# Splitting attention operands into hi and lo when they are made, not when they are loaded

## The chip, the cores and the metric

The kernel runs on one core of a Trainium2 chip. The metric is the device time of one execution in microseconds (us). The engines are named as the profile names them: PE multiplies matrices (PEld is its weight load), DVE is the vector engine, ACT the scalar engine, POOL is GpSimd, and SP only issues DMAs. Each engine works through its own instructions in a fixed order; an instruction that waits holds up all that stand behind it on the same engine, and this holds for SP and its DMAs too.

## What is computed

Two layers of a decoder trunk on 1024 tokens of width 1024. In each layer one input projection feeds four branches, which are gated, projected, merged by sigmoid gates, and added to the residual. Cut to the parts that the change touches:

```
q = (rms_norm(c_q) @ w_uq).reshape(S, 8 heads, 96)          # 64 plain + 32 rotary
k_nope, v = split((rms_norm(c_kv) @ w_ukv).reshape(S, 8, 128), 64)
k = concat(k_nope, k_rope shared by the heads)               # 96
q, k = rope(rms_norm(q)), rope(rms_norm(k))
y_b = causal softmax(q k^T / sqrt(96)) v                     # 8 heads, 1024 x 1024
# memory attention: 4 heads of 64, 256 memory tokens
q_m = rms_norm(h @ w_mq);  k_m, v_m = split(rms_norm(mem) @ w_kv)
y_m = softmax(q_m k_m^T / 8) v_m
```

## The kernel before

All data are fp32. A matrix product is taken in three fp32r passes: each operand x is split into hi = x rounded to fp32r and lo = x - hi, and the sum hi·hi + lo·hi + hi·lo is accumulated in PSUM. The helper `split` (L106 is its ACT copy that makes hi, L96 the subtraction that makes lo) does that on ACT plus either DVE or POOL. Where the source is a PSUM tile with a gain, ACT applies the gain and DVE makes lo in one scalar-tensor-tensor instruction.

The stages of a layer run in this order: statistics and the kv latent, memory queries (`mq_stage`), state-space input, `v_stage` and `k_stage` (keys and values of the latent attention), the state-space scan (`s5_scan`; `su` is its input read back from DRAM, `sz` and `sx` its DVE steps), memory keys and values, the state-space GLU (`gch`, `gcl` are its split operands, `glu` its result), `mem_attention` (4 heads), the q latent and `q_stage`, `attention` (8 heads in 4 blocks of 256 queries), and the merges.

Keys, queries, values and memory queries go through DRAM to change their layout. Before, each is stored as plain fp32 (`kscr`, `q2scr`, `vscr`, `qscr`), loaded into a raw tile `wr`, and split after each load: `fetch` makes `fh`/`fl` for keys and `wh`/`wl` for queries (hi on ACT, lo on POOL), `load_head` splits the values in the same way, and `mem_q` loads the same 64 rows twice, makes hi of both halves on ACT, and subtracts in the lower half on DVE. A head is loaded once per layer, three query blocks ahead.

Beside this, each layer has 18 background blocks (`background`, marked `bg` on PE): 48 matmuls of 128x512 each, 864 per layer, for the merge gates and branch gates. Their weights go through a raw tile `br` of which there is one, are converted by DVE (`bh`) and POOL (`bl`), and the product is taken up by DVE into `bgx`. Their loads and splits are ahead of the rest by priority (offset -800), and their matmuls have the lowest priority (offset -100000), so that a scheduler, which fixes the order of each engine when the kernel is built, puts them where it finds nothing else ready. Thus a change of any stage also changes where these matmuls stand. SP issues all DMAs.

In `k_stage` a small chain (`fk`, transposed by PE, through DRAM as `rkscr`) gives the factor tiles `rkb`, by which DVE multiplies the four key tiles `kraw`; POOL makes the rotary part `kro`, PE transposes it, ACT copies it out as `krt`; then all goes to `kscr`.

Of the kernel before, what the change touches and what calls it, by code (L numbers as in the profile page):

```python
# [17 lines left out]
P = 128  # L18
D = 1024
S = 1024  # L20
# [24 lines left out]
class Trunk:  # L45
# [174 lines left out]
    def setup(self):  # L220
# [37 lines left out]
        self.gscr = self.dp.tile([2, P, S], F32, name="gscr")  # L258
        self.qscr = self.dp.tile([2, P, S], F32, name="qscr")
        self.xscr = self.dp.tile([8, P, S], F32, name="xscr")  # L260

        self.kscr = self.dp.tile([96, 8, S], F32, name="kscr")
        self.vscr = self.dp.tile([8, P, 8, 64], F32, name="vscr")
        self.q2scr = self.dp.tile([96, 8, S], F32, name="q2scr")
        self.rkscr = self.dp.tile([64, P], F32, name="rkscr")
# [490 lines left out]
    def mq_stage(self, l):  # L756

        nc = self.nc
        ssm, sqs = self.ss(32, "ssm"), []
        for p in range(2):  # L760
            ps = self.cm(l, B_MQ + p, self.xg)
            sq = self.U("mqsq")
            self.act(sq, ps, AF.Square)
            q = self.U("mq")
            self.ts(q, ps, self.gmq[:, l:l + 1], MUL)
            nc.sync.dma_start(out=self.qscr[p], in_=q)
            sqs.append(sq)
        v = self.turn(self.quad([(self.sel2, sqs[i % 2][:, i // 2 * 512:i // 2 * 512 + 512]) for i in range(4)]))
        for i in range(4):
            nc.vector.tensor_copy(ssm.rearrange("p (u t h) -> p u t h", u=2, t=4)[:, i // 2, :, 2 * (i % 2):2 * (i % 2) + 2], v[:, :, 32 * i:32 * i + 2])  # L770
        pre = self.ss(32, "pre")
        nc.vector.tensor_copy(pre.rearrange("p (t h) -> p t h", t=8), self.rs.unsqueeze(2).to_broadcast([P, 8, 4]))
        r = self.inv_rms(ssm, 32, 64, pre)
        self.mqs = self.lp.tile([P, 32], F32, tag="mqs", name=self._n("mqs"))
        self.ts(self.mqs, r, M_SCALE, MUL)
# [93 lines left out]
    def q_stage(self, l, qacc):  # L869
# [4 lines left out]
        g = [t[:, l:l + 1] for t in (self.gq_x1, self.gq_x2)]  # L874
        dst = self.q2scr
        ps1 = self.block(w(0), self.cq, 6)
# [13 lines left out]
        for x, o in enumerate((o1, o2)):  # L890
            nc.sync.dma_start(out=dst[64 + 16 * x:80 + 16 * x].rearrange("f h s -> (f h) s"), in_=o)

# [10 lines left out]
        for p in range(4):  # L903
            ps = self.block(w(2 + p), self.cq, 6)
            sq = self.U("qsq")
            self.act(sq, ps, AF.Square)
            q = self.U("q")
            self.ts(q, ps, self.gqk[:, l:l + 1], MUL)
            for hh in range(2):
                nc.sync.dma_start(out=dst[0:64, 2 * p + hh], in_=q[hh * 64:hh * 64 + 64])  # L910
            sums(*sqs[p], first=p == 0)
# [24 lines left out]
    def v_stage(self, l):  # L936
# [3 lines left out]
        for t in range(8):  # L940
            ps = self.tr()
            xsl = slice(t * P, (t + 1) * P)
            for kt in range(2):
# [4 lines left out]
                self.mmr(ps, xh[:, xsl], wl[:, wsl], False, kt == 1)  # L948
            vt = self.U("vt")
            self.ts(vt[:, 0:512], ps, self.bkv[:, t:t + 1], MUL)  # L950
            nc.sync.dma_start(out=self.vscr[:, :, t, :].rearrange("h p d -> p h d"), in_=vt[:, 0:512].rearrange("p (h d) -> p h d", h=8))

    def k_stage(self, l, between):
# [44 lines left out]
        for x in range(2):  # L998
# [3 lines left out]
                    rk.rearrange("p (h t) -> p t h", h=8).unsqueeze(2).to_broadcast([P, 8, 16, 8]), MUL, eng=nc.gpsimd)  # L1002
            kt = self.U("krt")
            for tg in range(2):
                pt = self.tr()
                for j in range(4):
                    t = 4 * tg + j
                    nc.tensor.transpose(pt[:, j * P:(j + 1) * P], kro[:, t * P:(t + 1) * P], self.ident)
                self.act(kt[:, tg * 512:(tg + 1) * 512], pt, AF.Copy)
            nc.sync.dma_start(out=self.kscr[64 + 16 * x:80 + 16 * x].rearrange("f h s -> (f h) s"), in_=kt)  # L1010
        for p in range(4):
            self.tt(kraw[p], kraw[p], rbs[p], MUL)
            for hh in range(2):
                nc.sync.dma_start(out=self.kscr[0:64, 2 * p + hh], in_=kraw[p][hh * 64:hh * 64 + 64])  # L1014

# [10 lines left out]
    def load_head(self, h):  # L1026
        k = self.fetch(self.kscr[:, h])
        raw, v = self.wraw(), self.U("v", F32R)
        raw = raw[:, 0:512]
        self.nc.sync.dma_start(out=raw, in_=self.vscr[h].rearrange("p t d -> p (t d)"))  # L1030
        vv = v.rearrange("p (t k d) -> p k t d", t=8, k=2)
        self.split(vv[:, 0], vv[:, 1], raw.rearrange("p (t d) -> p t d", t=8), sub_eng=self.nc.gpsimd)
        return k, v

    def load_q(self, h):
        return self.fetch(self.q2scr[:, h], self.wpair())

# [95 lines left out]
    def mem_q(self, head):  # L1133

        nc = self.nc
        raw, q = self.wraw(), self.U("mq", F32R)
        hs = slice(head % 2 * 64, head % 2 * 64 + 64)
        for k in range(2):
            nc.sync.dma_start(out=raw[k * 64:k * 64 + 64], in_=self.qscr[head // 2, hs])
        self.act(q, raw, AF.Copy)  # L1140
        self.tt(q[64:128], raw[64:128], q[64:128].bitcast(F32), SUB)
        return q
# [532 lines left out]
```

## Time and profile before

| | us |
|---|---|
| median of three runs | 2448.62 (2446.93 to 2453.8) |
| the profiled execution | 2454.93 |
| its span, first to last instruction | 2453.0 |
| PE busy in it | 2338.4 (95%) |
| DVE, POOL, ACT busy | 1220.7, 776.5, 708.6 |

The mean granted PE clock of the profiled execution is 0.986 of 2.4 GHz. A row of the timeline gives the start, the duration, the engine, line and operation, out<-in, the count, and in brackets the idle time ahead of it with what ended that idle time. PE is busy nearly all the time, so its order and the waits in it are what is to be read.

### The profile page before, as it was taken

The page shows a single profiled execution, that of the slowest core. Times are in us where ns is not written, and L with a number is a line of the kernel's source. Part 1 is how long each engine was busy: PE and PEld are TensorE (multiplying, and loading weights), DVE is VectorE, ACT ScalarE, POOL GpSimd, SP SyncE. Part 2 cuts the span into 40 slices and gives each one's busy share as a digit, 9 for nine tenths or more (in the row PEclk, how much of TensorE's full clock was granted, in tenths as well). Part 3 has the DMA queues.
Part 4 walks back from the last instruction along what each step waited for, and adds up shares of the span by engine and source line. Part 5 has one row for each costly group of instructions (what it writes and reads, how often), then busy time and mean ns, then how long its engine had stood idle before and what let it go on. Part 6 is the DMA issues. An engine that isn't in the chain of part 4 may idle for free. (4 is left out here: it accounts for less than half of the span.)

```text
span 2453.0 us, 28729 instructions
## 1 busy us (share of the span) xinstructions
PE 2338.4 (95%) x11494; PEld 1885.2 (77%) x11494; DVE 1220.7 (50%) x1839; ACT 708.6 (29%) x1201; POOL 776.5 (32%) x606
## 2 busy tenths in 40 slices
PE   7998888999999999999999889999999999999999
PEld 5766677868788887887876667787778888788877
DVE  6454783266766224236244557714666652333341
ACT  3121253147753101101111213612577420111010
POOL 3533112432214124342445421233322132234411
PEclk9999999999999999999999999999999999999999
DMA  4226343242331113222432363313323211222342
GB/s 151 74 94 182 115 137 101 82 114 87 94 109 36 52 52 95 69 78 102 155 105 71 95 183 126 119 60 103 112 83 104 85 43 52 73 74 78 103 155 69
DMA packets 91701, 237.59 MB, mean 97 GB/s; under 512 B 25200, under 2 KB 34352, under 8 KB 91568
## 3 DMA queue, kind: packets, MB, share of 16 engines
q1 hardware_dynamic: 91568, 235.76, 30.1%
q8 instruction: 90, 1.47, 0.3%
q14 instruction: 43, 0.35, 0.0%
HBM read 175.27 MB, written 60.46 MB: 96 GB/s over the span
## 5 line engine op out<-in xcount | busy, mean ns | idle before, releaser
L96 POOL TENSOR_TENSOR wl<-wr,wh 128x1024 fp32r<-128x1024 f32 (+3 forms) x125 | 297.7, 2382 | 949.6 <-DVE wh L152 635.1
L152 DVE CAST wh<-wr 128x1024 fp32r<-128x1024 f32 (+2 forms) x110 | 79.1, 719 | 630.1 <-PE mm L176 555.3
L176 PE MATMUL mm<-xh,wh 128*128 128x512 f32 x1216 | 379.5, 392 | 10.1 <-ACT xh L106 9.7
L176 PE MATMUL mm<-xh,wl 128*128 128x512 f32 x1216 | 376.8, 391 | 0.7 <-POOL wl L96 0.7
L176 PE MATMUL mm<-xl,wh 128*128 128x512 f32 x1216 | 377.3, 391 | 0.0
L176 PEld LDWEIGHTS mm<-xh,wh 128*128 128x128 f32 x1216 | 227.8, 189 | 61.8 <-ACT xh L106 9.7
L176 PEld LDWEIGHTS mm<-xh,wl 128*128 128x128 f32 x1216 | 228.6, 188 | 49.9 <-POOL wl L96 1.6
L176 PEld LDWEIGHTS mm<-xl,wh 128*128 128x128 f32 x1216 | 228.9, 188 | 49.1 <-issue 0.8
L176 PE MATMUL bg<-xh,bh 128*128 128x512 f32 x576 | 228.1, 414 | 14.8 <-DVE bgx L96 14.8
L176 PE MATMUL bg<-xl,bh 128*128 128x512 f32 x576 | 225.8, 410 | 0.0
L176 PE MATMUL bg<-xh,bl 128*128 128x512 f32 x576 | 223.2, 407 | 0.6 <-POOL bl L96 0.5
L96 POOL TENSOR_TENSOR bl<-br,bh 128x1024 fp32r<-128x1024 f32 x36 | 95.3, 2647 | 309.0 <-DVE bh L152 209.9
L106 ACT ACTIVATE cmn<-cmn,bmh 128x1024 f32<-128x1024 f32 x44 | 50.7, 1152 | 457.2 <-DVE cmn L96 457.2
L176 PEld LDWEIGHTS bg<-xh,bh 128*128 128x128 f32 x576 | 111.9, 195 | 43.9 <-DVE bgx L96 23.3
L96 DVE TENSOR_TENSOR pT<-tr,pT 128x512 fp32r<-128x512 f32 x192 | 128.1, 686 | 30.7 <-ACT pT L106 28.5
L176 PE MATMUL pv<-pT,v 128*128 128x256 f32 x640 | 134.3, 308 | 7.3 <-DVE pT L96 3.8
L176 PEld LDWEIGHTS bg<-xh,bl 128*128 128x128 f32 x576 | 111.1, 193 | 24.4 <-issue 3.2
L176 PEld LDWEIGHTS pv<-pT,v 128*128 128x128 f32 x640 | 98.2, 190 | 40.1 <-DVE pT L96 14.5
L176 PEld LDWEIGHTS bg<-xl,bh 128*128 128x128 f32 x576 | 111.3, 194 | 21.4 <-issue 4.0
L106 ACT ACTIVATE pT<-tr 128x512 fp32r<-128x512 f32 x192 | 109.9, 596 | 46.2 <-PE tr L1100 36.0
L1059 DVE TENSOR_REDUCE mx<-mm 128x1 f32<-128x128 f32 (+7 forms) x128 | 96.1, 753 | 51.4 <-PE mm L176 49.9
L106 ACT ACTIVATE pr<-mm,nm,qs 128x128 f32<-128x128 f32 (+7 forms) x128 | 105.5, 832 | 0.7
(452 smaller groups left out, 4226.6 us busy)
## 6 DMA issues: line engine op xcount, KB each, us to landing
wr<-in_w_cm_dram SPq DMA_DIRECT2D x76, 512.0 KB, 3.6
br<-in_w_cm_dram SPq DMA_DIRECT2D x36, 512.0 KB, 3.7
bgscr<-bgx SPq DMA_DIRECT2D x20, 512.0 KB, 4.0
gate<-bgscr SPq DMA_DIRECT2D x20, 512.0 KB, 5.9
ysscr<-bgx SPq DMA_DIRECT2D x16, 512.0 KB, 2.6
br<-ysscr SPq DMA_DIRECT2D x16, 512.0 KB, 3.6
wr<-in_w_out_dram SPq DMA_DIRECT2D x16, 512.0 KB, 3.7
bgr<-riscr SPq DMA_DIRECT2D x24, 256.0 KB, 4.9
```

The source lines that it names most:

```text
L96: (eng or self.nc.vector).tensor_tensor(out=out, in0=x, in1=y, op=op)
L106: self.nc.scalar.activation(out, x, f, **k)
L152: self.nc.vector.tensor_copy(hi[:, :n], raw)
L176: self.nc.tensor.matmul(out, lhsT, rhs, start=start, stop=stop)
L1059: nc.vector.reduce_max(out=mx, in_=ps[:, 0:n], axis=AX.X)
```

## The change

Keys, queries, values and memory queries are split when they are made. The DRAM tiles hold hi and lo, and the loads go straight into the operand tiles; `fetch` is left for the gated branches alone.

```
-        self.qscr = self.dp.tile([2, P, S], F32, name="qscr")
+        self.qscr = self.dp.tile([2, 2, P, S], F32, name="qscr")
-        self.kscr = self.dp.tile([96, 8, S], F32, name="kscr")
-        self.vscr = self.dp.tile([8, P, 8, 64], F32, name="vscr")
-        self.q2scr = self.dp.tile([96, 8, S], F32, name="q2scr")
+        self.kscr = [self.dp.tile([96, 8, S], F32, name="kscr" + x) for x in "hl"]
+        self.q2scr = [self.dp.tile([96, 8, S], F32, name="q2scr" + x) for x in "hl"]
+        self.vscr = self.dp.tile([8, P, 8, 2, 64], F32, name="vscr")
...
-            q = self.U("mq")
-            self.ts(q, ps, self.gmq[:, l:l + 1], MUL)
-            nc.sync.dma_start(out=self.qscr[p], in_=q)
+            q = self.U("mqh", F32R), self.U("mql", F32R)
+            self.split(*q, ps, gain=self.gmq[:, l:l + 1])
+            for k in range(2):
+                nc.sync.dma_start(out=self.qscr[k, p], in_=q[k].bitcast(F32))
...
         for x, o in enumerate((o1, o2)):
-            nc.sync.dma_start(out=dst[64 + 16 * x:80 + 16 * x].rearrange("f h s -> (f h) s"), in_=o)
+            part = self.U("qrh", F32R), self.U("qrl", F32R)
+            self.split(*part, o, sub_eng=nc.gpsimd)
+            for k in range(2):
+                nc.sync.dma_start(out=self.q2scr[k][64 + 16 * x:80 + 16 * x].rearrange("f h s -> (f h) s"), in_=part[k].bitcast(F32))
...
-            vt = self.U("vt")
-            self.ts(vt[:, 0:512], ps, self.bkv[:, t:t + 1], MUL)
+            vt = self.U("vt", F32R).rearrange("p (h k d) -> p k h d", h=8, k=2)
+            self.split(vt[:, 0], vt[:, 1], ps.rearrange("p (h d) -> p h d", h=8), gain=self.bkv[:, t:t + 1])
...
         for p in range(4):
             self.tt(kraw[p], kraw[p], rbs[p], MUL)
-            for hh in range(2):
-                nc.sync.dma_start(out=self.kscr[0:64, 2 * p + hh], in_=kraw[p][hh * 64:hh * 64 + 64])
+            part = self.U("kh", F32R), self.U("kl", F32R)
+            self.split(*part, kraw[p], sub_eng=nc.gpsimd)
+            for k in range(2):
+                for hh in range(2):
+                    nc.sync.dma_start(out=self.kscr[k][0:64, 2 * p + hh], in_=part[k][hh * 64:hh * 64 + 64].bitcast(F32))
...
     def load_head(self, h):
-        k = self.fetch(self.kscr[:, h])
-        raw, v = self.wraw(), self.U("v", F32R)
...
+        k, v = [self.U("k" + x, F32R) for x in "hl"], self.U("v", F32R)
+        for z, src in zip(k, self.kscr):
+            self.nc.sync.dma_start(out=z[0:96].bitcast(F32), in_=src[:, h])
+        self.nc.sync.dma_start(out=v.bitcast(F32), in_=self.vscr[h].rearrange("p t k d -> p (t k d)"))
...
     def mem_q(self, head):
-        raw, q = self.wraw(), self.U("mq", F32R)
+        q = self.U("mq", F32R)
         hs = slice(head % 2 * 64, head % 2 * 64 + 64)
         for k in range(2):
-            nc.sync.dma_start(out=raw[k * 64:k * 64 + 64], in_=self.qscr[head // 2, hs])
-        self.act(q, raw, AF.Copy)
-        self.tt(q[64:128], raw[64:128], q[64:128].bitcast(F32), SUB)
+            nc.sync.dma_start(out=q[k * 64:k * 64 + 64].bitcast(F32), in_=self.qscr[k, head // 2, hs])
         return q
```

The queries of `q_stage` get the same edit as the memory queries, and `krt` becomes the pair `krh`, `krl`. On SP the number of issues grows from 545 to 621.

The order of the engines moves with it. In the next two lists stands what POOL does around `kro` in the key stage of the first layer; `br`, `bh`, `bl` are a background block's raw, hi and lo weights. Before:

```order
L96 TENSOR_TENSOR bl_942<-br_939,bh_941 128x1024
L96 TENSOR_TENSOR kro_2113<-krot_1439,qs_2092 128x1024
L96 TENSOR_TENSOR kro_2129<-krot_1439,qs_2092 128x1024
L96 TENSOR_TENSOR bl_1003<-br_1000,bh_1002 128x1024
L96 TENSOR_TENSOR bl_1064<-br_1061,bh_1063 128x1024
```

After, on POOL at the same place:

```order
L96 TENSOR_TENSOR bl_944<-br_941,bh_943 128x1024
L96 TENSOR_TENSOR bl_1005<-br_1002,bh_1004 128x1024
L96 TENSOR_TENSOR kro_2129<-krot_1441,qs_2108 128x1024
L96 TENSOR_TENSOR kro_2149<-krot_1441,qs_2108 128x1024
L96 TENSOR_TENSOR kl_2171<-kraw_1913,kh_2170 128x1024
L96 TENSOR_TENSOR kl_2180<-kraw_1930,kh_2179 128x1024
L96 TENSOR_TENSOR kl_2189<-kraw_1947,kh_2188 128x1024
L96 TENSOR_TENSOR kl_2198<-kraw_1964,kh_2197 128x1024
L96 TENSOR_TENSOR bl_1066<-br_1063,bh_1065 128x1024
```

A second background split (bl_1005) now stands ahead of `kro`, and the next one (bl_1066) behind four new `kl`. On SP, the stores of the keys in the first layer stood before the change like this, with the scan's input `su` and the next weights `br` behind them:

```order
L1010 DMA kscr<-krt_2115 128x1024
L1010 DMA kscr<-krt_2131 128x1024
L1014 DMA kscr<-kraw_1905 64x1024 x2
L1014 DMA kscr<-kraw_1922 64x1024 x2
L1014 DMA kscr<-kraw_1939 64x1024 x2
L1014 DMA kscr<-kraw_1956 64x1024 x2
L620 DMA su_2157<-cscr 128x8x128
L149 DMA br_1000<-in_w_cm_dram 128x1024
```

After, from the first `kh` on, behind four stores of krh and krl:

```order
L1022 DMA kscrh<-kh_2170 64x1024 x2
L1022 DMA kscrl<-kl_2171 64x1024 x2
L1022 DMA kscrh<-kh_2179 64x1024 x2
L1022 DMA kscrl<-kl_2180 64x1024
L149 DMA br_1063<-in_w_cm_dram 128x1024
L1022 DMA kscrl<-kl_2180 64x1024
L1022 DMA kscrh<-kh_2188 64x1024 x2
L149 DMA br_1124<-in_w_cm_dram 128x1024
L1022 DMA kscrl<-kl_2189 64x1024 x2
L1022 DMA kscrh<-kh_2197 64x1024 x2
L1022 DMA kscrl<-kl_2198 64x1024 x2
L620 DMA su_2205<-cscr 128x8x128
```

The key stores are 20 instead of 10, two loads of background weights stand among them (another, br_1002, stands ahead of the `rkb` loads), and `su` is last. The third place is SP around the first memory query of the second layer. Before, the loads of its first two heads (`wr`) had been issued long ahead, and behind the stores of `glu` stood those of the other two:

```order
L149 DMA br_12052<-in_w_cm_dram 128x1024
L686 DMA gscr<-glu_11520 128x1024
L686 DMA gscr<-glu_11537 128x1024
L1139 DMA wr_11789<-qscr 64x1024 x2
L1139 DMA wr_11887<-qscr 64x1024 x2
```

After, where mq_11726 is the first head's query, read by the first matmul of the memory scores:

```order
L149 DMA br_12232<-in_w_cm_dram 128x1024
L1148 DMA mq_11726<-qscr 64x1024
L686 DMA gscr<-glu_11572 128x1024
L686 DMA gscr<-glu_11589 128x1024
L1148 DMA mq_11726<-qscr 64x1024
L149 DMA wr_12478<-in_w_cm_dram 128x1024
L1290 DMA bgy_11655<-gscr 128x1024
L1299 DMA ysscr<-bgx_11599 128x1024
L1148 DMA mq_11747<-qscr 64x1024 x2
```

The first head's query is now loaded by two DMAs that stand around the `glu` stores. In the first layer its two loads stand behind the stores of the rotary tables (`tabscr<-ropes`, `tabscr<-ropec`).

On PE the 11384 matmuls and transposes are the same in number and shape; background matmuls move. Between the `kro` transposes and the scan's `su` products there were 51 of them, now 119; from the first `gch` product to the first memory score there were 107 in the first layer and 48 in the second, now 69 and 16; in the second layer's attention there were 318, now 238, as in the first layer before and after (242 and 238); and 13 and 11 stood at the end of a background block inside the merges, now none.

## Rows read from the trace of the kernel before

**Rows 1.** Busy time by engine, head of the page (us, share of span, instructions).

```profile
PE 2338.4 (95%) x11494; PEld 1885.2 (77%) x11494; DVE 1220.7 (50%) x1839; ACT 708.6 (29%) x1201; POOL 776.5 (32%) x606
```

**Rows 2.** What PE waited for: total us, times, longest us.

```profile
PE tr L660 <- DVE sx L96: 13.1, 5, 4.1
PE tr L176 <- DVE vt L100: 10.6, 4, 3.3
...
PE mm L176 <- DVE mq L96: 5.9, 5, 3.0
PE mm L628 <- DMA su<-cscr: 5.0, 2, 2.5
...
PE mm L176 <- DVE q L96: 2.6, 1, 2.6
PE mm L176 <- POOL fl L96: 1.9, 2, 1.6
```

**Rows 3.** Stretches: us, busy of PE, PEld, DVE, ACT, POOL; PEclk, DMA, GB/s.

```profile
180.00:400.00 220.00, 189.54 (x914) 147.56 (x913) 144.06 (x219) 76.55 (x140) 50.31 (x54) 0.97 0.46 143
500.00:560.00 60.00, 54.00 (x282) 40.97 (x281) 42.63 (x73) 30.51 (x59) 20.15 (x9) 0.97 0.39 110
1380.00:1580.00 200.00, 176.39 (x868) 138.70 (x868) 126.76 (x205) 76.86 (x141) 61.31 (x87) 0.97 0.45 139
1700.00:1760.00 60.00, 52.82 (x260) 40.71 (x258) 43.24 (x71) 24.85 (x49) 20.11 (x9) 0.94 0.44 132
```

**Rows 4.** PE, key stage to scan, first layer: start us, us, operation, idle before.

```profile
221.74 1.03 PE L1008 MATMUL tr<-ident,kro 128*128 128x128 f32 x8
...
222.85 0.40 PE L176 MATMUL bg<-xl,bh 128*128 128x512 f32 x1
223.08 0.40 PE L176 MATMUL bg<-xh,bh 128*128 128x512 f32 x1
...
239.30 1.97 PE L628 MATMUL mm<-su,wst 128*64 128x128 f32 x32 [2.51 <-DMA su<-cscr]
```

**Rows 5.** POOL in the key stage of the first layer.

```profile
213.36 2.39 POOL L96 TENSOR_TENSOR bl<-br,bh 128x1024 fp32r<-128x1024 f32 x1 [20.28 <-issue]
215.71 7.15 POOL L96 TENSOR_TENSOR kro<-krot,qs 128x1024 f32<-128x1024 f32 x2
241.61 2.38 POOL L96 TENSOR_TENSOR bl<-br,bh 128x1024 fp32r<-128x1024 f32 x1 [18.75 <-DVE bh L152]
```

**Rows 6.** DVE in the key stage of the first layer.

```profile
215.47 1.36 DVE L96 TENSOR_TENSOR kraw<-kraw,rkb 128x1024 f32<-128x1024 f32 x1 [2.24 <-DMA rkb<-rkscr]
217.74 6.21 DVE L96 TENSOR_TENSOR kraw<-kraw,rkb 128x1024 f32<-128x1024 f32 x2 [0.91 <-DMA rkb<-rkscr]
...
240.78 0.69 DVE L152 CAST bh<-br 128x1024 fp32r<-128x1024 f32 x1 [3.12 <-DMA br<-in_w_cm_dram]
```

**Rows 7.** SP in the key stage of the first layer.

```profile
225.55 6.95 SPq L1014 DMA_DIRECT2D kscr<-kraw  x8
232.59 1.05 SPq L620 DMA_DIRECT2D su<-cscr  x1
233.74 1.05 SPq L149 DMA_DIRECT2D br<-in_w_cm_dram  x1
```

**Rows 8.** SP ahead of the memory scores, first and second layer.

```profile
332.61 0.32 SPq L839 DMA_DIRECT2D tabscr<-ropec  x1
...
1528.99 1.45 SPq L686 DMA_DIRECT2D gscr<-glu  x2
```

**Rows 9.** PE at the first memory scores, first and second layer.

```profile
334.93 0.36 PE L176 MATMUL mm<-mk,mq 128*128 128x256 f32 x1 [1.97 <-DVE mq L96]
...
1526.80 0.62 PE L176 MATMUL mm<-gch,wl 128*128 128x512 f32 x2
...
1531.50 0.35 PE L176 MATMUL mm<-mk,mq 128*128 128x256 f32 x1 [0.23 <-DVE mq L96]
```

**Rows 10.** Loads of the memory queries: count, KB each, median us to landing.

```profile
wr<-qscr SPq DMA_DIRECT2D x16, 256.0 KB, 4.2
```

More of the change, by code (lines that the diff above doesn't have):

```diff
@@ L874, in q_stage @@
         g = [t[:, l:l + 1] for t in (self.gq_x1, self.gq_x2)]
-        dst = self.q2scr
         ps1 = self.block(w(0), self.cq, 6)
@@ L906, in q_stage @@
             self.act(sq, ps, AF.Square)
-            q = self.U("q")
-            self.ts(q, ps, self.gqk[:, l:l + 1], MUL)
-            for hh in range(2):
-                nc.sync.dma_start(out=dst[0:64, 2 * p + hh], in_=q[hh * 64:hh * 64 + 64])
+            q = self.U("qh", F32R), self.U("ql", F32R)
+            self.split(*q, ps, gain=self.gqk[:, l:l + 1])
+            for k in range(2):
+                for hh in range(2):
+                    nc.sync.dma_start(out=self.q2scr[k][0:64, 2 * p + hh], in_=q[k][hh * 64:hh * 64 + 64].bitcast(F32))
             sums(*sqs[p], first=p == 0)
@@ L948, in v_stage @@
                 self.mmr(ps, xh[:, xsl], wl[:, wsl], False, kt == 1)
-            vt = self.U("vt")
-            self.ts(vt[:, 0:512], ps, self.bkv[:, t:t + 1], MUL)
-            nc.sync.dma_start(out=self.vscr[:, :, t, :].rearrange("h p d -> p h d"), in_=vt[:, 0:512].rearrange("p (h d) -> p h d", h=8))
+            vt = self.U("vt", F32R).rearrange("p (h k d) -> p k h d", h=8, k=2)
+            self.split(vt[:, 0], vt[:, 1], ps.rearrange("p (h d) -> p h d", h=8), gain=self.bkv[:, t:t + 1])
+            nc.sync.dma_start(out=self.vscr[:, :, t].rearrange("h p k d -> p h (k d)"), in_=vt.rearrange("p k h d -> p h k d").bitcast(F32))
     def k_stage(self, l, between):
@@ L1002, in k_stage @@
                     rk.rearrange("p (h t) -> p t h", h=8).unsqueeze(2).to_broadcast([P, 8, 16, 8]), MUL, eng=nc.gpsimd)
-            kt = self.U("krt")
+            kt = self.U("krh", F32R), self.U("krl", F32R)
             for tg in range(2):
@@ L1008, in k_stage @@
                     nc.tensor.transpose(pt[:, j * P:(j + 1) * P], kro[:, t * P:(t + 1) * P], self.ident)
-                self.act(kt[:, tg * 512:(tg + 1) * 512], pt, AF.Copy)
-            nc.sync.dma_start(out=self.kscr[64 + 16 * x:80 + 16 * x].rearrange("f h s -> (f h) s"), in_=kt)
+                self.split(*[z[:, tg * 512:(tg + 1) * 512] for z in kt], pt)
+            for k in range(2):
+                nc.sync.dma_start(out=self.kscr[k][64 + 16 * x:80 + 16 * x].rearrange("f h s -> (f h) s"), in_=kt[k].bitcast(F32))
         for p in range(4):
             self.tt(kraw[p], kraw[p], rbs[p], MUL)
-            for hh in range(2):
-                nc.sync.dma_start(out=self.kscr[0:64, 2 * p + hh], in_=kraw[p][hh * 64:hh * 64 + 64])
+            part = self.U("kh", F32R), self.U("kl", F32R)
+            self.split(*part, kraw[p], sub_eng=nc.gpsimd)
+            for k in range(2):
+                for hh in range(2):
+                    nc.sync.dma_start(out=self.kscr[k][0:64, 2 * p + hh], in_=part[k][hh * 64:hh * 64 + 64].bitcast(F32))
     def fetch(self, src, pair=None, raw=None, sub_eng=None):
@@ L1026, in load_head @@
     def load_head(self, h):
-        k = self.fetch(self.kscr[:, h])
-        raw, v = self.wraw(), self.U("v", F32R)
[L1029 to L1032, printed above, removed]
+        k, v = [self.U("k" + x, F32R) for x in "hl"], self.U("v", F32R)
+        for z, src in zip(k, self.kscr):
+            self.nc.sync.dma_start(out=z[0:96].bitcast(F32), in_=src[:, h])
+        self.nc.sync.dma_start(out=v.bitcast(F32), in_=self.vscr[h].rearrange("p t k d -> p (t k d)"))
         return k, v
     def load_q(self, h):
-        return self.fetch(self.q2scr[:, h], self.wpair())
+        q = self.wpair()
+        for z, src in zip(q, self.q2scr):
+            self.nc.sync.dma_start(out=z[0:96].bitcast(F32), in_=src[:, h])
+        return q
     def attn_scores(self, head, b, qt, kT):
```

## The prediction, made before the change was run

> **What bounds the kernel now.** I read the busy times first. PE works 2338.4 of 2453.0 us [rows 1], so about 115 us of idle PE is all that a better order can win, and every new wait of PE costs its full length, since the number of matmuls stays as it is. Next come the waits of PE, where the reader is to see two things: that the operands which this change touches appear there with little (memory queries 5.9 us, values 10.6, the first queries 2.6, the first keys 1.9), and that more of the list belongs to the scan behind the key stage (`sx` 13.1, `su` 5.0) [rows 2]. Then the windows say where the idle time lies: the stretch from key stage to memory scores has 220 - 189.5 = 30.5 us in the first layer and 200 - 176.4 = 23.6 in the second, the attention start 60 - 54.0 = 6.0 and 60 - 52.8 = 7.2 [rows 3]. Last, the timeline of each engine in the key stage, because the order there changes most [rows 4 to 7].
>
> The sum is made against the profiled execution, which took 2454.93 us, 6.3 above the median of 2448.62. I add the difference to the median.
>
> **What is removed.** The three splits at the load of each of the 16 heads go from ACT and POOL. Two of POOL's are of the size of one `bl`, 2.38 us [rows 5], so some 16 x 2 x 2.4 = 76 us of POOL time go, and the half-size one of the values besides. Nearly all of it lay beside PE work: PE waited for keys 1.9 us and for queries 2.6 us in all [rows 2]. What this is worth is read at the attention start, where the first head's load and split are exposed. After a load-to-use chain without the two conversions I expect the idle of that window to go, also because the clock of 0.97 and 0.94 there [rows 3] would not fall after such gaps: -6 in the first layer and -7 in the second, **-13**. Lower bound for this gain is 0, if the q stores, now two per tile, land as late as the splits ended; upper bound the -13 and some 2 us of clock.
>
> In the value stage, PE waited 10.6 us for `vt` [rows 2]. The DVE step keeps its length, ACT gets one more of the same size ahead of it; but the order now has a background matmul pair or more between the groups. I take **-2** (bounds -8 and +8, all covered or doubled).
>
> Inside attention and in the merges the relief of ACT and POOL and the 24 background matmuls that no longer end a block in a merge (24 x 0.23 us, the spacing of two of them [rows 4], is 5.5) fill idle time elsewhere: **-4** and **-4** (bounds 0 and -9 for each). Behind the first memory score, the waits for `mq` that are left (5.9 less 1.97 and 0.23 [rows 2, 9], 3.7) go with the two splits: **-3** (0 to -4).
>
> **What the key stage costs.** Here are three steps, all in the first layer's trace, and I take the second layer to be alike.
>
> First, `kro`. POOL made it from 215.71 to 222.86 [rows 5], and PE took the first half's transposes at 221.74 without waiting [rows 4], 2.5 us after it was ready (215.71 + 3.58 = 219.3). Now POOL does another `bl` first, 2.39 us, whose `bh` stands on DVE behind the first `kraw` multiply, which waits for `rkb` until 215.47 and ends at 216.83 [rows 6], then behind two background evictions of 1.3 us together and a cast of 0.69. So `bl` runs from about 218.9 to 221.3, the first `kro` from 221.3 to 224.9, the second to 228.5. PE reaches the first transposes with one background matmul less than before: a wait of 3.2, and some 0.8 at the second: +4 (bounds 0, if `rkb` lands earlier, and +8, if the weights' load ahead of `rkb` on SP delays it).
>
> Second, the background weights. Before, SP issued 8 key stores in 6.95 us, 0.87 each, then `su` at 232.59 and `br` at 233.74 [rows 7]; that `br` was cast on DVE at 240.78 after a wait for its landing [rows 6], its `bl` came at 241.61 [rows 5], and it was ready for PE at 244.0. Now the next load, br_1063, stands behind 4 stores of `krh`, `krl` (the second pair from about 230.5) and 7 more, 232.4 + 7 x 0.83 = 238.2. With the 7.0 us from issue to cast (240.78 - 233.74) it is cast at 245.2 and split by 248.3. It also has to wait for four `kl` on POOL, 4 x 2.38 from 228.5 or 238.0, which decides nothing. PE by then has used up what is ready: the 119 matmuls hold 2.5 blocks, of which the ones in hand end near 237.8 to 239. A wait of +9 (bounds 0, if the block in hand is longer than I count, and +14, if the next load, br_1124, which waits for that split, makes a second gap).
>
> Third, `su` is issued last, near 253, but PE comes to it only after 119 matmuls (27 us at 0.23) and the wait above, so its 2.5 us go; and the cast that stood among the `sz` steps on DVE is gone, so `sx` comes 3 us sooner. Against it stands a background eviction that is now behind a cast in DVE's order, +2.6. Sum for one layer 4 + 9 - 2.5 - 3 + 2.6 = +10; for both, **+20** (bounds -11 and +40).
>
> At this place DVE and POOL also hinder each other. Beside `bl` and the start of `kro` one `kraw` multiply took 1.36 us, beside `kro` two took 6.21, 3.1 each [rows 6]. The four `kl` now follow `kro` on POOL, and by this row three `kraw` would take 1.75 us more each, 5.2 us in all. The weights land later than this, so my sum leaves it out; it belongs to the dear case below. The Trainium skill, in "GPSIMD Engine Reference", section "Key points", says that GpSimd shares its SBUF interfaces with VectorE and contends with vector instructions that have two SBUF inputs. The multiplies have two such inputs, and by that rule the slow pair is this and not chance; the trace agrees, with 3.1 against 1.36. By the rule the sum would be up to 2 x 5.2 = 10 us higher, without it not.
>
> **What the first memory score costs.** Before, its raw load was issued long ahead and only ACT and DVE steps were late: waits of 1.97 and 0.23 [rows 9]. Now the load into the operand tile stands late on SP. First layer: behind `tabscr<-ropec`, issued at 332.61 [rows 8] when ACT has its table; two issues and 4.2 us of landing [rows 10] later is 337.7. PE has 38 background matmuls less between `gch` and the scores, 38 x 0.23 = 8.7, so it arrives at 332.96 - 8.7 = 324.3. If the tables stay where they are, it waits 13.4; if they move earlier with the 15 matmuls dropped ahead of the second `gch`, 10. Less the old 1.97: +8 to +11. Second layer: the second half is issued behind the `glu` stores, 1528.99 + 1.45 [rows 8], and lands at 1534.9. PE ends its `gch` products at 1527.3, and the scores follow at once, where 17 matmuls stood before [rows 9]: a wait of 7.6, and up to 3 more where the second `gch` comes earlier and has to wait for ACT. Sum, less 0.23: +7.5 to +10.5. I take 9 in each, **+18** (bounds 0, if SP reaches these loads early because the stores ahead are done sooner, and +26, with the lower clock after such gaps).
>
> **Sum.** 20 + 18 - 13 - 2 - 4 - 4 - 3 = **+12 us**, or 2460.6 by the median: 2461.
>
> **The rivals.**
> - Faster: the loads are in time. The background weights land before PE runs dry, and SP reaches the memory queries earlier than I think, because `tabscr` and `glu` shift with PE. For it speaks that before the change the same placing left only small waits there, 1.97 and 0.23 [rows 9]. Against it speaks the one `br` tile, which lets no second load be in flight. Key stage +2 and scores +2 per layer, and the gains as above: 8 - 26 = -18, 2431.
> - No change: the gaps are half of mine, key stage +6 and scores +6 per layer, 24 against 26: -2, 2447. PE's work is the same, so what fills a gap earlier is lacking later. It decides from gaps of 4 us and less at `br` and `mq`.
> - Dear: the mechanism is the doubled key stores on one queue. They put br_1124 and `su` 20 us later than before; if the landings rise as well, and the contention of `kl` and `kraw` comes on top, the key stage costs 17 per layer and the scores 13: 60 less 26 is +34, 2483. It decides if the bytes in the key stage, and not the order, set the time of the stores.
> - That the change does not do what it says can be left out, since the order shows each split and store where the text of it puts them.
>
> **How the numbers follow.** The forecast (2452 to 2472) 0.42, faster 0.25, no change 0.20, dear 0.13. A measurement of this kernel tells 0.3% (7.3 us) from no change. The faster case gives the 0.25 for faster; the case of no change and a little of the forecast's low end 0.23 for the same; the rest 0.52 for slower. The range reaches to 2435 at the low end, near the faster case, and to 2486, just past the dear one. The likeliest case's own range is 2452 to 2472.
>
> **What would show it.** A wait of PE on `bl` or on its weights of some 9 us per layer between `kro` and `su`, with `su`'s wait gone; a wait on `kro` of 3 to 4; a wait of PE on the DMA of `mq` of 8 to 13 in the first and 7 to 11 in the second layer; no idle at the attention start. I am wrong if PE's list of waits shows no `mq<-qscr` load and no `bl` of more than 4 us, or if the attention windows keep their 6 and 7 us.

## The result, and the profile after

The changed kernel takes 2515.72 us (median of 2513.98 to 2517.23) against 2448.01: the ratio is 1.0265 [1.0247, 1.0283], some 66 us slower. The forecast was 2461, with a range from 2435 to 2486.

The profiled execution of after spans 2512.3 us, 59.3 more than that of before. Busy times at the head of its page, in the columns of [rows 1]:

```profile
PE 2357.2 (94%) x11494; PEld 1899.7 (76%) x11494; DVE 1204.3 (48%) x1839; ACT 697.9 (28%) x1185; POOL 704.4 (28%) x570
```

PE is idle for 2512.3 - 2357.2 = 155.1 us, 40.5 more than the 114.6 of before. Its busy time is 18.8 us longer for the same 11494 matmuls and transposes (this is the count of both traces; 11384 ahead of the prediction is too low). That goes with the lower clock: the mean granted clock is 0.976 after 0.986. These two make up the 59.3.

The waits of PE, in the columns of [rows 2], first `bgx` before, then all after:

```profile
PE bg L176 <- DVE bgx L96: 14.8, 16, 4.2
```

```profile
PE bg L176 <- DVE bgx L96: 30.2, 21, 9.7
PE mm L176 <- DMA mq<-qscr: 9.4, 2, 8.8
PE mm L176 <- ACT pr L106: 9.0, 8, 1.2
PE mm L176 <- ACT gch L106: 8.9, 4, 2.6
...
PE tr L660 <- DVE sx L96: 7.8, 8, 1.7
...
PE tr L176 <- DVE vt L103: 6.3, 4, 2.7
...
PE tr L1012 <- POOL kro L96: 3.8, 1, 3.8
PE bg L176 <- DVE bh L152: 3.1, 2, 1.5
...
PE bg L176 <- POOL bl L96: 2.8, 2, 1.5
...
PE mm L628 <- DMA su<-cscr: 1.8, 2, 1.6
```

`vt`, `sx` and `su` have become smaller, as forecast, and `q` and `fl` are gone. `kro` is there with 3.8, the background weights (`bh`, `bl`) only with 5.9 in all, and the load of `mq` with 8.8 in the second layer. Much larger is the wait on `bgx`, 30.2 against 14.8 before, with one of 9.7. The rest is spread over `pr`, `gch` and `pT`, steps in the middle of chains.

The same row of the first layer's merge shows how much of the loss the first layer has, before and after:

```profile
1150.56 0.61 PE L176 MATMUL mm<-mh,wh 128*128 128x512 f32 x2
```

```profile
1190.46 0.61 PE L176 MATMUL mm<-mh,wh 128*128 128x512 f32 x2
```

It comes 39.9 us later; that is two thirds of the 59.3. I follow the first layer.

**Key stage.** PE there, after, to be read beside [rows 4]:

```profile
228.45 1.97 PE L1012 MATMUL tr<-ident,kro 128*128 128x128 f32 x8 [3.79 <-POOL kro L96]
...
252.94 0.50 PE L176 MATMUL bg<-xh,bh 128*128 128x512 f32 x1 [1.53 <-DVE bh L152]
...
255.45 0.73 PE L176 MATMUL bg<-xh,bl 128*128 128x512 f32 x2 [1.31 <-POOL bl L96]
...
267.29 1.97 PE L628 MATMUL mm<-su,wst 128*64 128x128 f32 x32 [1.57 <-DMA su<-cscr]
```

The wait on `kro` is 3.79, as worked out (3.2 and 0.8). The weights cost 1.53 and 1.31 instead of 9: PE's stock of ready blocks lasted to 251.4, not to 238 or 239. `su` is used at 267.29 instead of 239.30. SP, beside [rows 7]:

```profile
243.16 1.05 SPq L149 DMA_DIRECT2D br<-in_w_cm_dram  x1
...
255.43 0.34 SPq L149 DMA_DIRECT2D br<-in_w_cm_dram  x1
...
260.80 1.10 SPq L620 DMA_DIRECT2D su<-cscr  x1
```

The first `br` is issued at 243.16 (forecast 238.2), the next waits to 255.43 for POOL's split of the first, and with six more key stores behind it holds `su` to 260.80 (forecast 253). So far the working holds within some us. The contention of DVE and POOL that it left out is seen too, in two multiplies in a row, and POOL's `bl` beside them:

```profile
221.54 1.22 DVE L96 TENSOR_TENSOR kraw<-kraw,rkb 128x1024 f32<-128x1024 f32 x1
223.26 2.83 DVE L96 TENSOR_TENSOR kraw<-kraw,rkb 128x1024 f32<-128x1024 f32 x1 [0.50 <-DMA rkb<-rkscr]
```

```profile
221.75 3.25 POOL L96 TENSOR_TENSOR bl<-br,bh 128x1024 fp32r<-128x1024 f32 x1 [11.88 <-DVE bh L152]
```

The first multiply began 0.21 us ahead of `bl` and took 1.22 us, no more than one with POOL idle (1.23 at 218.60), while `bl` took 3.25 instead of 2.38. The second began while `bl` ran and took 2.83. Each time the one that began second took longer.

**From the scan to the end of memory attention** is where most of the first layer's loss arises. The table takes the same matmuls before and after (start in us) and the number of background matmuls that the traces have ahead of them. A delay by background matmuls done earlier is no loss, so the last column takes 0.23 us off for each that is more; it is an estimate.

| | before | after | later by | more `bg` ahead | left |
|---|---|---|---|---|---|
| first layer, first `su` product | 239.30 | 267.29 | 28.0 | 96 | 5.9 |
| first `gch` product | 299.84 | 333.20 | 33.4 | 96 | 11.3 |
| first memory score | 334.93 | 372.81 | 37.9 | 58 | 24.5 |
| last transposes of memory attention | 396.3 | 434.6 | 38.3 | 17 | 34.4 |
| merge, the row above | 1150.56 | 1190.46 | 39.9 | 0 | 39.9 |
| second layer, first `su` product | 1451.66 | 1518.75 | 67.1 | 96 | 45.0 |
| first `gch` product | 1512.36 | 1580.19 | 67.8 | 96 | 45.7 |
| first memory score | 1531.50 | 1606.00 | 74.5 | 64 | 59.8 |
| last transposes of memory attention | 1585.4 | 1666.7 | 81.3 | 80 | 62.9 |
| end of the span | 2453.0 | 2512.3 | 59.3 | 0 | 59.3 |

In both layers the largest step is from `gch` to the first memory score, 13 and 14 us. In the first layer memory attention adds 10, in the second 3. Windows of the first layer before (`gch` to memory scores, memory attention) and the same two after, in the columns of [rows 3]:

```profile
300.00:335.00 35.00, 30.82 (x132) 24.21 (x132) 27.82 (x25) 11.89 (x11) 5.12 (x2) 1.00 0.40 140
335.00:395.00 60.00, 51.56 (x271) 40.76 (x272) 43.87 (x58) 36.34 (x93) 10.87 (x4) 0.97 0.44 133
```

```profile
334.00:373.00 39.00, 26.07 (x93) 19.42 (x92) 25.77 (x25) 9.74 (x9) 6.68 (x3) 0.78 0.43 148
373.00:435.00 62.00, 48.98 (x242) 38.82 (x241) 34.57 (x51) 33.84 (x90) 4.60 (x2) 0.86 0.29 86
```

These windows have 132 + 271 = 403 matmuls in 95 us before, and 93 + 242 = 335 in 101 us after. With 68 matmuls less, 15.6 us of PE work at 0.23, they still take 6 us longer. The granted clock is 0.78 and 0.86, against 1.00 and 0.97. What PE does in the middle of memory attention after the change:

```profile
385.24 1.09 PE L176 MATMUL tr<-pT,mv 128*128 128x512 f32 x4
...
389.87 0.39 PE L176 MATMUL bg<-xh,bl 128*128 128x512 f32 x1
...
403.22 1.25 PE L176 MATMUL tr<-pT,mv 128*128 128x512 f32 x4 [3.81 <-DVE pT L96]
...
408.74 2.07 PE L176 MATMUL tr<-pT,mv 128*128 128x512 f32 x4 [1.69 <-DVE pT L96]
...
419.09 0.80 PE L176 MATMUL bg<-xh,bh 128*128 128x512 f32 x1 [3.30 <-DVE bgx L96]
```

```profile
405.00:419.00 14.00, 8.50 (x36) 6.83 (x36) 6.79 (x10) 5.62 (x18) 0.00 (x0) 0.62 0.43 133
```

Between 389.87 and 419.09 there is not one background matmul. PE waits for the memory branch's own steps. After these gaps its granted clock falls for a time to the lower of the clock's two levels, 1.2 of 2.4 GHz (0.62 in the mean of the window from 405 to 419): a group of four products takes 2.07 us at 408.74, where the same took 1.09 at 385.24. Between the first score and the last transposes of this layer's memory attention the traces have 86 background matmuls before and 45 after, so fewer are left to fill its gaps, and 119 instead of 51 stand between `kro` and `su`. In the second layer this isn't so (82 and 98); there the short stretch is the one ahead of the scores, with 16 instead of 48.

The longest wait, the 9.7 on `bgx`, comes ahead of the memory scores. On DVE and PE:

```profile
347.85 4.50 DVE L103 SCALAR_TENSOR_TENSOR glu<-glu,yc 128x1024 f32<-128x1024 f32 x2
...
356.49 0.69 DVE L96 TENSOR_TENSOR bgx<-bg,rsb 128x512 f32<-128x512 f32 x1
```

```profile
357.24 0.79 PE L176 MATMUL bg<-xh,bh 128*128 128x512 f32 x1 [9.70 <-DVE bgx L96]
```

The background eviction `bgx` at 356.49 stands on DVE behind both `glu` steps and five steps of the rotary tables, and PE's PSUM buffer is not free before. The forecast had a wait of 8 to 11 at this place, but for the load of `mq`. In the second layer it is that load, behind the `glu` stores as worked out:

```profile
1598.25 3.61 SPq L686 DMA_DIRECT2D gscr<-glu  x2
1601.90 0.47 SPq L1148 DMA_DIRECT2D mq<-qscr  x1
```

```profile
1606.00 0.55 PE L176 MATMUL mm<-mk,mq 128*128 128x256 f32 x1 [8.84 <-DMA mq<-qscr]
```

**Attention.** The start gained, and the interior lost. First the first layer's interior before, then after the first layer's start and interior and the second layer's start (columns as above):

```profile
560.00:725.00 165.00, 162.60 (x1037) 133.43 (x1037) 118.10 (x168) 121.02 (x266) 38.79 (x19) 1.00 0.29 90
```

```profile
540.00:600.00 60.00, 57.34 (x317) 44.13 (x316) 35.01 (x73) 30.43 (x66) 2.38 (x1) 1.00 0.57 158
594.00:771.00 177.00, 166.46 (x1037) 137.18 (x1038) 119.27 (x169) 109.55 (x249) 4.79 (x2) 0.98 0.39 110
1760.00:1820.00 60.00, 57.30 (x289) 43.30 (x287) 30.75 (x65) 26.34 (x48) 4.22 (x2) 1.00 0.64 187
```

At the start 2.7 us of idle are left in each layer instead of 6.0 and 7.2. Inside the first layer's attention as many matmuls, 1037, take 177 us instead of 165, with 10.5 us of idle instead of 2.4.

### The profile page after: what moved, and what is told of

Its sections match the earlier page's. It is cut to its first block, busy times and chain, and to the rows that moved or that the text cites. A ratio compares the mean times of both kernels' runs of the same rounds, so it can differ in the third digit from the quotient of the medians.

```text
span 2512.3 us, 28839 instructions
## 1 busy us (share of the span) xinstructions
PE 2357.2 (94%) x11494; PEld 1899.7 (76%) x11494; DVE 1204.3 (48%) x1839; ACT 697.9 (28%) x1185; POOL 704.4 (28%) x570
## 5 line engine op out<-in xcount | busy, mean ns | idle before, releaser
L96 POOL TENSOR_TENSOR wl<-wr,wh 128x1024 fp32r<-128x1024 f32 (+2 forms) x109 | 260.3, 2388 | 1004.8 <-DVE wh L152 494.5
L176 PE MATMUL bg<-xh,bh 128*128 128x512 f32 x576 | 234.2, 421 | 33.3 <-DVE bgx L96 30.2
```

What stands on the lines that cost most here:

```text
L96: (eng or self.nc.vector).tensor_tensor(out=out, in0=x, in1=y, op=op)
L176: self.nc.tensor.matmul(out, lhsT, rhs, start=start, stop=stop)
```

## The experiments

The ratios are to the kernel before, with their 95% intervals. Three theories were held against each other at first: F (the scan comes late, background matmuls fill the time and are missing later), D, later called M (direct waits, as in the forecast), and a rival, N at first (the order of the whole), then W (the change frees the raw tiles `wr`, so that later weights are loaded and split too early). Of each edit only the lines that tell the runs apart are shown.

**One part alone.** Each keeps the change's hunks for one operand, the others are as before.

```
e1: +        self.kscr = [self.dp.tile([96, 8, S], F32, name="kscr" + x) for x in "hl"]  (k_stage, load_head)
e2: +        self.qscr = self.dp.tile([2, 2, P, S], F32, name="qscr")                    (mq_stage, mem_q)
e3: +        self.vscr = self.dp.tile([8, P, 8, 2, 64], F32, name="vscr")                (v_stage, load_head)
e4: +        self.q2scr = [self.dp.tile([96, 8, S], F32, name="q2scr" + x) for x in "hl"] (q_stage, load_q)
```

e1: 

> Only the keys are split when they are made; values, queries and memory queries as before. Theory F (late scan): the doubled key stores and the four kl hold back su, PE fills the time with background matmuls (48 more per layer ahead of su), and these are missing later, where memory attention has its own pace; the loss goes with their number, half of the 96 of the full change, so about +30 us. Theory D (direct waits, as forecast): the key stage costs +10 per layer and the first keys' wait goes: +15 to +20. Rival N (the stages do not add up; the loss comes from the order as a whole): any value, within 7 us of before is possible.

e2: 

> Only the memory queries are split when they are made. Theory F: nothing is moved ahead of su, so only the late load of the first memory query shows: +5 to +10. Theory D: a wait for the load of mq of 9 us in each layer, less 3 us of waits inside memory attention: +15. Rival N: within 7 us of before.

e3: 

> Only the values are split when they are made. Theories F and D: the value stage is covered by background matmuls (13 more of them ahead of the key stage), the attention load loses one split: 0, at most 5 us either way. Rival N: slower by over 10 us, if the ACT step ahead of the DVE step in the value stage is exposed.

e4: 

> Only the queries are split when they are made; the order ahead of the q stage stays word for word. Theories F and D: the attention start gains (the waits on the first queries and keys and the lower clock after them): -5 to -10. Rival N (the doubled stores and loads delay attention): slower by 5 to 10.

Measured: 1.0005 [0.9995, 1.0016], 0.9977 [0.9965, 0.9989], 1.0018 [1.0005, 1.0031] and 0.9994 [0.9984, 1.0005]. The medians are +1.2, -4.5, +3.0 and -2.2 us from 2447.49; their sum is -2.6. The sums that theories F and D gave for the keys and for the memory queries are all wrong, and the 5 to 10 us that both saw in the queries did not come (-2.2 is not clear of zero). Only the values came out as they said. No part costs more than 3 us by itself, and the loss is one of the combination.

**One part left out.** The same hunks, taken back one at a time.

```
e5: -        self.kscr = [self.dp.tile([96, 8, S], F32, name="kscr" + x) for x in "hl"]
e6: -        self.qscr = self.dp.tile([2, 2, P, S], F32, name="qscr")
e7: -        self.vscr = self.dp.tile([8, P, 8, 2, 64], F32, name="vscr")
e8: -        self.q2scr = [self.dp.tile([96, 8, S], F32, name="q2scr" + x) for x in "hl"]
```

e5: 

> Everything but the keys is split when made. The parts alone add up to about -3 us, so the +67 of the whole come from a combination. Theory F (late scan, then too few background matmuls): 48 matmuls more ahead of su instead of 96 and no key stores in front of su, so most of the loss goes: within 10 us of before. Rival W (freed wr tiles: with no raw loads of memory queries and heads, later weights are loaded and split ahead of the glu and memory chains): the loss stays, +40 or more, since values, queries and memory queries still free the tiles.

e6: 

> Everything but the memory queries. Theory F: 65 matmuls more ahead of su, and the raw loads of the memory queries stand early: +10 to +30. Rival W: the wr tiles are in use by the memory queries as before, so the loss goes: within 10 us of before.

e7: 

> Everything but the values. Theory F: 38 matmuls more ahead of su in the first layer, 48 in the second, about as with keys alone: within 15 us of before. Rival W: the values' split stands at the start of attention, late; the loss stays, +40 or more.

e8: 

> Everything but the queries. The order ahead of the q stage is that of the full change (96 more matmuls ahead of su, 62 and 22 more up to the first memory score). Theory F: the loss stays, +55 to +70. Rival W: the same up to the q stage. If it falls to under +20, the loss sits in q stage and attention, against both.

Measured: 1.0117 [1.0091, 1.0144], 1.0027 [1.0017, 1.0036], 1.0058 [1.0039, 1.0078], 1.0215 [1.0192, 1.0239]; +29, +6, +13 and +53 us. Each of keys, values and memory queries is needed for the whole loss; without the memory queries nearly all of it is gone. e7 speaks against W. e5 and e6 speak against F in its plain form: without the keys there is no doubled key store in front of `su` and 29 us stay, and e6 falls to +6, where F had +10 to +30 and W had within 10. Neither theory has all four.

**The two late loads.** e9 loads `su` of the second scan ahead of the key stage, e10 puts the first two memory query loads ahead of the GLU, e11 does both, e12 moves two background blocks behind memory attention.

```
e9:              st[1] = self.s5_tables(l, 1)
    +            sus.append(self.s5_load(1))
                 self.k_stage(l, lambda: self.v_stage(l))
e10:             self.mem_kv(l)
    +            self.mq_ahead = {h: self.mem_q(h) for h in range(2)}
                 glu()
e12: -NB1 = 9
     +NB1 = 7
```

e9: 

> The full change, with the load of the second scan's input su issued ahead of the key stage instead of behind its stores; background matmuls ahead of su fall from 384 to 260 in the first layer (288 before the change). Theory F (the scan comes late behind the 20 key stores, background matmuls fill the time and are missing in the glu and memory stages, where PE then idles and its clock falls): most of the loss goes, +20 to +30 left of +67. Theory M (direct waits at the first memory score, for the late mq load and the background eviction there): falls by 10 at most, +55. Theory W (freed wr tiles): unchanged, +60 or more.

e10: 

> The full change, with the loads of the first two memory queries called ahead of the glu instead of behind it. The order ahead of the scan stays (384 matmuls ahead of su). Theory F: only the wait for mq goes, +50 or more left. Theory M: the waits of 9 to 10 in each layer go with what follows from them, +40 or less. Theory W: +60 or more.

e11: 

> Both of these. Theory F and M together: within 15 us of before. Theory W: +40 or more.

e12: 

> The full change with two background blocks fewer ahead of memory attention (7 and 3 instead of 9 and 1; they move into the q stage and attention): 336 matmuls ahead of su, 68 between the first memory score and the q rows as in the full change. Theory F, as a lack of filler where the chain is slow: not better, +60 or more, since fewer are ahead and as few are in memory attention. If the loss were PE work put in front of the chain, moving 96 matmuls behind it would give 10 us or more back.

Measured: e9 1.0096 [1.0076, 1.0116], e10 1.0165 [1.0142, 1.0189], e11 1.0032 [1.0018, 1.0046], e12 1.0243 [1.0222, 1.0264]; +26, +42, +9 and +62 us. The early `su` takes about 40 us away, the early `mq` about 25, both about 58: they nearly add up. Neither edit moves a load alone, since the scheduler places all anew: with e9 PE does the second scan's first products at 178.4, early in the value stage and ahead of the `kro` transposes (267.29 after), with 149 background matmuls ahead of them instead of 384; with e10 no background matmul stands between `gch` and the first memory score (69 after). So the runs show where the loss hangs, and not that the lateness of the two loads alone makes it. e12 shows that fewer background matmuls ahead hardly help. PE then waits for the chain instead, 21.5 us for `gch` and 16.1 for `su` (8.9 and 1.8 with the full change):

```profile
PE mm L176 <- ACT gch L106: 21.5, 4, 8.4
PE mm L628 <- DMA su<-cscr: 16.1, 3, 8.4
```

Memory attention of e9, beside the windows above:

```profile
350.00:407.00 57.00, 53.89 (x284) 43.16 (x284) 40.08 (x57) 35.02 (x91) 7.16 (x3) 0.97 0.38 117
```

It has 284 matmuls in 57 us at a clock of 0.97, where after had 242 in 62 at 0.86. Between its first score and its last transposes stand 95 background matmuls, against 45.

**Are these repairs or gains?**

```
e13: the kernel before, with e9's edit
e14: e2 and e4 together (queries and memory queries)
e15: e14 with e10's edit          e16: e14 with e9's and e10's
e17: e14 and the keys, with both edits
```

e13: 

> The kernel before, without any of the change, with the second scan's su loaded ahead of the key stage. If the early load is a gain by itself and no repair, it gives here what it gave in the full change, -40 us. Theory F: before the change su came only 2.5 us late in each layer, so it gives -5 to 0, or a small loss where the background order shifts.

e14: 

> Only queries and memory queries are split when made: no key stores added, 288 matmuls ahead of su as before. If the parts are independent: -4.5 - 2.2 = -7 us. Theory F: about that, since su isn't delayed; a loss of over 5 us would show that the late mq load hurts without the late scan.

e15: 

> The same with the first two memory query loads called ahead of the glu. Theory M: 5 to 15 us better than without the early load. Theory F: 0 to 5 better, since the late load costs much only when the scan is late too.

e16: 

> The same with su early as well. If both early loads are repairs only: no better than queries and memory queries alone, -5 to -8 from before. If they are gains of their own: -15 or more.

e17: 

> Keys, queries and memory queries split when made (values as before), with both early loads. Between e16 (no keys, 7 us below before) and e11 (values too, 9 us above). If the key stores still cost once su is ahead of them (POOL's kl and the waits on kro of 2 to 4 us): +3 to +10 against before. If the keys cost nothing then and the values carry the rest of e11: -5 or lower.

Measured: e13 1.0025 [1.0011, 1.0039], e14 1.0067 [1.0043, 1.0092], e15 1.0077 [1.0053, 1.0101], e16 0.9963 [0.9950, 0.9977], e17 1.0073 [1.0053, 1.0094]. The early `su` is no gain without the change (+7). e14 is a miss: two parts that alone measure -4.5 and -2.2 us lose 16 together, and the early `mq` (e15) doesn't mend it. The trace of e14 shows another wait for a late load, in attention (DVE, then PE):

```profile
601.01 1.23 DVE L103 SCALAR_TENSOR_TENSOR bgx<-bgx,bgy 128x1024 f32<-128x1024 f32 x1 [4.73 <-DMA bgy<-ybscr]
```

```profile
604.03 1.01 PE L176 MATMUL pv<-pT,v 128*128 128x256 f32 x3 [4.28 <-DVE pT L96]
```

A background gate step stands on DVE ahead of attention's `pT` and waits 4.73 us for the load of `bgy`, which SP issued among the next head's loads. Inside the first layer's attention DVE waits for `bgy` 11.7 us in all with e14; it is 3.8 after and 1.3 before, so a small part of this stands in the full change too. e17 is a miss too: the keys cost some 26 us against e16, although `su` is early. SP and PE there:

```profile
262.57 0.33 SPq L149 DMA_DIRECT2D br<-in_w_cm_dram  x1
...
263.44 0.59 SPq L669 DMA_DIRECT2D yscr<-sy  x1
264.13 1.25 SPq L699 DMA_DIRECT2D mraw<-in_memT_dram  x1
```

```profile
271.27 1.22 PE L176 MATMUL mm<-wh,mh 128*128 128x512 f32 x2 [5.51 <-ACT mh L106]
```

The scan's result `yscr` and the memory tokens `mraw` have taken `su`'s place behind the key stores and two loads of weights, the second of which holds SP until 262.57; PE then waits 5.51 for `mh`. e16 is 9 us or so below before by the ratio, near the -5 to -8 of two repairs and short of the -15 of gains of their own; it is not told apart from e2 (0.9977 [0.9965, 0.9989]).

**The buffers.** Each `U(...)` tile takes one of the 38 buffers of the ring `NU`. The change asks for more: two tiles for one at each memory query, rotary key and query, and two beside `kraw` at each key, each held until its store has landed. The values ask for none: `vt` is one tile before and after. If the tiles are the cause, less of the ring for the kernel before should do the same:

```
-NU = 38
+NU = 34
```

> The kernel before, with 34 instead of 38 buffers in the ring U from which the change takes its additional tiles (two instead of one for each memory query, rotary key, key and query). Nothing else is changed: no split moved, no store added. The scheduler then places 384 background matmuls ahead of su in the first layer, 416 - 288 = 128 more up to the second layer's order of the full change (512 at gch, 1392 at the memory scores), just as in the full change. Theory P (the change loses because its added tiles delay the allocations behind them and so reorder the layer): +30 or more, with PE starved in memory attention. Theory S (the added stores and kl on SP and POOL themselves cost the time): within 10 us of before, since none are added here.

Measured: 1.0309 [1.0295, 1.0323], +77 us, with no split moved and no store added. PE's waits in it:

```profile
PE bg L176 <- DVE bgx L96: 28.0, 23, 5.2
PE tr L176 <- DVE vt L100: 22.1, 2, 11.8
```

Its windows from `gch` to the first memory score and of memory attention, in the first layer, to be read beside those of after:

```profile
334.00:370.00 36.00, 27.40 (x86) 20.31 (x86) 24.96 (x23) 10.85 (x11) 3.21 (x1) 0.76 0.36 136
370.00:433.00 63.00, 55.81 (x285) 44.90 (x286) 44.03 (x64) 39.29 (x96) 12.27 (x5) 0.95 0.43 134
```

The order of the background matmuls is as with the full change, 384 ahead of `su` and 512 at `gch`. The wait on `bgx` (28.0) and the stretch from `gch` to the first score (clock 0.76) are much like those of the full change. The rest isn't: memory attention runs at 0.95, so that it was not starved as theory P said, and the value stage loses far more (`vt` 22.1 against 6.3). By the same estimate as in the table 14 us are lost ahead of `kro` in the first layer, where the full change loses 1.

So a shortage of buffers alone, with no store added, can reorder a layer and cost as much. That the change loses through its tiles is not shown. Against it speaks e7: leaving out the values, which ask for no more tiles, takes 53 of the 66 us away. Nor is theory S ruled out as a part, that the stores and the `kl` cost time: leaving out the keys (e5) takes away 37 us, tiles and stores together. After, e8 and e18 are the kernels with 384 background matmuls ahead of `su` and 512 at `gch`, and they lose 66, 53 and 77 us; e1, e5, e6 and e7 have 326 to 353 ahead of `su` and lose 1 to 29. That is a link and no proof: e12 loses 62 with 336.

## Why the prediction was wrong

The direction was right and the size was not: +12 forecast, +66 measured, far beyond the range.

The step that failed comes with the third of the key stage: "`su` is issued last, near 253, but PE comes to it only after 119 matmuls (27 us at 0.23) and the wait above, so its 2.5 us go." The times in it were nearly right (260.80, and 1.57 us of wait left). Wrong was to let the matter end there. The 119 matmuls are no reserve: 68 of them were moved there from behind, and the scan, the GLU and memory attention start 25 to 38 us later with the work gone that used to cover their gaps. For the lack of it the sum has no term. It counts the stretch from `gch` to the memory scores as one wait of 9, has nothing from the scan to `gch`, and books gains of 3 behind the first memory score and of 4 inside attention. The prediction had the thought: its case of no change says "what fills a gap earlier is lacking later", and gives it no price.

In the first layer `sx` ends 25.7 us later with 96 more background matmuls ahead of it, some 22 us of work, so the key stage itself cost about 4, less than the 10 of the sum. The last transposes of memory attention come 38.3 later with only 17 more ahead, 3.9 us of work: about 30 us were lost in between. Inside the first layer's attention 12 more were lost.

Point by point:
- Attention start -13: its idle fell by 3.3 and 4.5. Counted as in the table above, with the clock, the two windows gained about 5 and 7 us, so this term held. The interior was forecast at -4 and cost 12 us in the first layer alone. This term is among those farthest off, and its cause is open but for the waits on `bgy`.
- `vt` -2: its wait fell by 4.3.
- `kro` +4: 3.79 in the first layer, held. In the second the list has no wait on POOL's `kro`.
- Background weights +9 in each layer: 2.8 in the first; the count of ready blocks was too low.
- `su` and `sx` -5.5 in each layer: their waits fell by 3.2 and 5.3 for both layers together.
- First memory score +9: 8.84 in the second layer for the reason given; in the first a wait of 9.7 stands ahead of it for another reason, an eviction behind the rotary tables on DVE, and that the number is near the forecast is luck. What I left out is what followed. The early loads of `mq` give 25 us in the whole kernel, order and all, against my 18.
- The contention of POOL and DVE was put into the dear case only. One multiply took 2.83 instead of 1.22, and `bl` 0.9 us more: a matter of a few us.
- The dear rival had the right place, stores on one queue ahead of `su`, and the right sign; it was priced at +34 because it too counted waits. Its point of decision, that the bytes set the time of the stores, is not borne out by the trace: the key stores land in 4.4 us before and in 4.5 and 4.3 after (medians of 16 from issue, rows below), and SP stood 8.8 us behind one `br` (246.6 to 255.43). It is the order.
- The faster rival rested on the loads being in time; with two of the four parts and both loads early (e16) it comes true in direction, 9 us instead of 18.
- The signs of being wrong did not come up: `mq` waits 8.8, and the attention windows lost their idle. They tested the waits that the sum names, not the stages that it leaves out.

```profile
kscr<-kraw SPq DMA_DIRECT2D x16, 256.0 KB, 4.4
```

```profile
kscrh<-kh SPq DMA_DIRECT2D x16, 256.0 KB, 4.5
kscrl<-kl SPq DMA_DIRECT2D x16, 256.0 KB, 4.3
```

Shown by runs: the parts do not add up; putting the two loads ahead, with the order that follows, takes away about 58 of the 66 us; a ring of 34 buffers costs the kernel before as much, in part at other places. Shown by the trace alone: the gaps and the clock between `gch` and the end of memory attention. Argued and not shown: that the tiles of the change are what reorders it. Left open: why the values matter so much, why e14, e15 and the full change lose inside the first layer's attention beyond the waits named, and how many buffers each part takes at the moment that counts. The full change with a larger ring, which would tell, was not tried.

## What to carry to other kernels

Count a change's tiles as well as its instructions: where a scheduler places work by the tiles that are free, four buffers fewer reordered whole layers here, and what each part costs alone says nothing of the sum. Background work that fills a delay is spent, not saved; look at which later stage lived on it, and price that stage too. In a queue in order, a load that is late passes its lateness on to whatever stands behind it, so moving one load forward shows the next.

## What the runs showed of the hardware

The clock of PE costs beside the waits: from `gch` to the end of the first layer's memory attention the granted clock was 0.78 and 0.86 (1.00 and 0.97 before), with one single wait above 4 us, and the whole kernel's busy time is 18.8 us longer for the same matmuls. DVE and POOL held each other up, and the one that began second paid: a `kraw` multiply took 1.22 us when it began 0.21 us ahead of `bl` and 2.83 when it began behind, and `bl` 3.25 instead of 2.38. The Trainium skill, "GPSIMD Engine Reference", section "Key points", names vector instructions with two SBUF inputs among those that contend with GpSimd. The trace agrees with it by these numbers.
